# Forty early expert groups instead of forty-four, an earlier A load, and seam arithmetic on VectorE, in a two-block network with dense experts

## The chip, the cores and the metric

The kernel runs on one core of one Trainium2 chip. The metric is device microseconds of one execution. All matrix products are float32 work done as three products of rounded float32 parts (high and low halves), so that each weight tile costs a split into two tiles before it can be multiplied.

## What is computed

Two residual blocks over 512 tokens of width 1024. Each has a token mixer (gated linear attention in the first; retention and stick-breaking attention in the second) and then a PEER layer: eight heads pick 16 of 16,384 single-neuron experts by product keys. Cut to what matters here:

```python
def peer(h, w_query, sub_keys, expert_down, expert_up):          # second block; the first is alike
    qry = (ht @ w_query).reshape(T, 8, 2, 128)
    sub_scores = einsum('thpc,hpkc->thpk', qry, sub_keys)
    top_s, top_i = top_k(sub_scores, 16)                          # per half key
    best_s, best_c = top_k(all sums of two halves, 16)            # 16 experts per head
    gate = softmax(best_s)
    a = einsum('pd,ped->pe', x, expert_down[ids])                 # "U" products
    return einsum('pe,ped->pd', gelu(a) * gate, expert_up[ids])   # "V" products
```

Between the blocks stand two RMS norms with gains, and the second block's norms are modulated by scale, shift and gate rows that come from a small product of a condition vector.

## The kernel before

**The experts.** The first 128 tokens fetch their chosen rows: GpSimd issues 256 indirect DMAs of 128 rows (`Gathered.fetch`, L864), 128 of U and 128 of V, and VectorE consumes each with one 128x1024 operation (`Gathered.use`, L876 for U, L883 for V). The other 384 tokens are computed densely over all experts. The experts stand in 128 tiles of 128, taken in 64 pairs ("expert groups" of `GRP` = 2). For each tile, TensorE makes 24 matmuls of 128x384 into `pu` (`Inward.run`, L908), ScalarE takes the GELU of it into `A` (L915), and later A times the gate matrix `G`, which gives `W` (L1102 on VectorE), weighs the V rows: 36 matmuls of 128x512 for a pair into six accumulators `acc` (`mm3`, L119 to L121).

**Two stages.** In the early stage VectorE picks the experts and builds one-hot matrices, from which TensorE makes the gate matrix (`oh`, `og`, `pg`), in 32 steps for each of three token tiles. Between these steps TensorE runs U products: `PICK_MM`, `QUAD_MM` or `LAST_MM` matmuls at each step. `NEARLY` of the 64 pairs have their U products there, and their A tiles are written to DRAM (`ad`). In the dense stage, iteration p multiplies pair p. Pairs whose A came early are loaded back (`load_a(p + LA)`, L1071). The other pairs ("fresh" ones) get their U products in the dense stage, eight matmuls after each of the six parts of the iteration p for which p + 2 is fresh; since 144 of these matmuls (`OVER`, three pairs' worth) are done ahead, the last three fresh iterations find nothing left to multiply. The gathers left over are spread over the dense stage by weights: an iteration with p + 2 fresh counts `FW` = 4, another 1, up to pair 57.

**What sets the order.** Instructions are issued in the order of the code, one queue per engine. Weights and rows come by DMAs that SP issues in order, each behind the release of the buffer it fills; at most eight of SP's transfers are under way in the program's own semaphores, since each also waits for the eighth before it. `A` has 12 buffers (`GRP * AB`). ScalarE makes each high half, VectorE each low half (L264 for U, L1088 for V and W).

**The seams.** Between the dense stage of the first block and the second block's first products, `Between.rows` norms each token tile twice (L1731 to L1745); between the second mixer and its experts, `add` (L1796, L1797) and `rms_rows` (L197, L199) do the same; at the end `Last.rows` (L1829, L1833) adds the residual. GpSimd does some of the elementwise operations of these, chosen by `HGP`, `SHB`, `SHP` and the half; it also takes every power of -0.5. In iteration 33 of the first block the modulation table goes through DRAM (`modd`, L1708) and is read back as rows (L1565) on SP's queue.

Of the kernel before, what the change touches and what calls it, by code (L numbers as in the profile page):

```python
# [17 lines left out]
ALU = mybir.AluOpType  # L18
# [5 lines left out]
NT = 4  # L24
# [8 lines left out]
JUMPS = (16, 8, 5, 4, 3, 2, 2, 2)  # L33
SUBE = lambda nc: nc.vector
GRP = 2
NEARLY = 44
NHELD = 0
FRONT = 4
MLAG = 1
# [9 lines left out]
MT = 16  # L49
FW = 4  # L50
WB = (0, 2)
LA = 2
AB = FRONT + 2
HGP = (0, 1, 2)
ADA = (8, 7, 7)
ADA0 = 0
SHB = (0,)
HALVES = ((0, 512), (512, 1024))
S1 = 2
YR = 2  # L60
# [14 lines left out]
M2_LAG = 4  # L75
SB = 1
SPE = 0
SHP = 3
RP_ACT = (0, 1)
PICK_MM = 40  # L80
QUAD_MM = 20
LAST_MM = 16
PK = 2
LAG = 3
DOT = (2, 2, 1)
# [7 lines left out]
class K:  # L93
# [83 lines left out]
    def rms_rows(self, pool, t, row, gain, out=None, shift=None, known=None):  # L177

        nc = self.nc
        rs = pool.tile([128, 1], F32, name=f"rs{t}", tag="rrs", bufs=NT)
        j = pool.tile([128, D], F32, name="rsj", tag="rsj", bufs=1)
        o = 512 if known is not None else 0
        self.square_mean(rs, j[:, o:], row[:, o:])
        yield
        if known is None:
            nc.vector.tensor_scalar(rs, rs, EPS, None, op0=ALU.add)
        else:
            nc.vector.scalar_tensor_tensor(rs, rs, EPS, known, op0=ALU.add, op1=ALU.add)  # L190
        nc.gpsimd.tensor_tensor(rs, rs, self.mhalf, op=ALU.pow)
        if out is None:
            out = pool.tile([128, D], F32, name=f"xn{t}", tag="xn", bufs=NT)
        yield
        for c in HALVES:
            c = slice(*c)
            nc.vector.scalar_tensor_tensor(out[:, c], row[:, c], rs, gain[:, c], op0=ALU.mult, op1=ALU.mult)  # L197
            if shift is not None:
                (nc.gpsimd if t < SHP else nc.vector).tensor_tensor(out[:, c], out[:, c], shift[:, c], op=ALU.add)  # L199
        yield  # L200
        self.turn(out, t)

# [1338 lines left out]
def body(tc, a, out, stop=None):  # L1541
    nc = tc.nc
    with ExitStack() as ctx:
        k = K(ctx, tc, a)
        c = k.const
# [55 lines left out]
        with ExitStack() as c1:  # L1601
# [40 lines left out]
            gf = gain_row(ada, a["norm_f_g"], "gf")  # L1642
# [6 lines left out]
            h = [pool.tile([128, D], F32, name=f"h{t}") for t in range(NT)]  # L1649
# [24 lines left out]
        sh = []  # L1674
# [37 lines left out]
        class Between:  # L1712
# [14 lines left out]
            def rows(self, t, parts):  # L1727
                h, n = self.h[t], D // len(parts)
                for i, p in enumerate(parts):
                    s = h[:, i * n:(i + 1) * n]  # L1730
                    nc.vector.tensor_tensor(s, s, p, op=ALU.add)  # L1731
                yield
                v = ada.tile([128, 2], F32, name="v", tag="v", bufs=NT)
                k.square_mean(v[:, 0:1], self.junk, h)
                hg = self.tile("wide")
                (nc.gpsimd if t in HGP else nc.vector).tensor_tensor(hg, h, gf, op=ALU.mult)
                yield
                k.square_mean(v[:, 1:2], self.junk, hg)
                yield
                nc.vector.tensor_scalar(v[:, 0:1], v[:, 0:1], EPS, None, op0=ALU.add)  # L1740
                nc.vector.scalar_tensor_tensor(v[:, 1:2], v[:, 0:1], EPS, v[:, 1:2], op0=ALU.mult, op1=ALU.add)
                nc.gpsimd.tensor_tensor(v, v, k.mhalf.to_broadcast([128, 2]), op=ALU.pow)
                yield
                nc.vector.scalar_tensor_tensor(h, hg, v[:, 1:2], cs, op0=ALU.mult, op1=ALU.mult)
                (nc.gpsimd if t in SHB else nc.vector).tensor_tensor(h, h, sh[0], op=ALU.add)  # L1745
                yield
                if t == 0:
                    yield
                k.turn(h, t)
                self.out.append((t, hg, v))  # L1750
# [18 lines left out]
        with ExitStack() as c1:  # L1769
            mp = pool_of(c1, "mp2")  # L1770
            MH = mp.tile([128, NK, T], F32R, name="MH")
            ML = mp.tile([128, NK, T], F32R, name="ML")
            cos, sin = mp.tile([128, T], F32, name="cos"), mp.tile([128, T], F32, name="sin")
            rv = [mp.tile([128, 512], F32, name=f"rv{t}") for t in range(NT)]
            for t, p in end.first:
                by = lambda x: x.rearrange("p (h d) -> p h d", h=8)
                nc.vector.tensor_tensor(by(rv[t]), by(p), grow[:, t, :, None].to_broadcast([128, 8, 64]), op=ALU.mult)
            ms.close()
            with ExitStack() as c3:
                pool = pool_of(c3, "mx2")  # L1780
                prod = Product(k, ws, 28, MH, ML, OUT_ORDER)
                mixer2(k, c3, pool, rv, cos, sin, MH, ML, ws, prod)
            ms.enter_context(tc.manual_schedule())
            pool = pool_of(c1, "po2")
            h = [pool.tile([128, D], F32, name=f"h{t}") for t in range(NT)]
            hn = pool_of(c2, "gt2", side="right").tile([128, D], F32, name="ghn")
            for t in range(NT):
                nc.sync.dma_start(h[t], x2[t])
            g1, shift, scale = (row(pool.tile([128, D], F32, name=f"row{i}"), i) for i in (2, 3, 4))
            steps = Steps()  # L1790

            def add(half):
                def f(t, p):
                    c_ = slice(half * 512, (half + 1) * 512)
                    m = pool.tile([128, 512], F32, name="m", tag="m", bufs=2)
                    nc.vector.tensor_tensor(m, p, g1[:, c_], op=ALU.mult)  # L1796
                    (nc.vector if half else nc.gpsimd).tensor_tensor(h[t][:, c_], h[t][:, c_], m, op=ALU.add)  # L1797
                    if half:
                        steps.add(k.rms_rows(pool, t, h[t], scale, hn if t == 0 else None, shift, k.half_mean(pool, t, h[t][:, :512])))
                        steps.step()  # L1800
                return f

            for _ in prod.parts([3]):
                pass
            for t in range(NT):
                add(0)(t, prod.outs[t])
            ws.ready(33)
            ah = Ahead(k, a["peer_w_query_2"], a["peer_sub_keys_2"], a["peer_down_2"], 4)
            token_rows(k, ws, 32, MH, ML, ["acc", "acc", "mm", "mm"], add(1), tail=True, order=OUT_ORDER)
            first = by_halves(k, ah.ws, steps)  # L1810
            for t in range(NT):
                nc.sync.dma_start(x3[t], h[t])

        class Last:
# [10 lines left out]
            def rows(self, t, parts):  # L1825
                y, n = self.tile("wide"), D // len(parts)
# [3 lines left out]
                yield  # L1830
                for i in range(2):
                    s = slice(i * 512, (i + 1) * 512)
                    (nc.vector if t == NT - 1 or i else nc.gpsimd).tensor_tensor(y[:, s], y[:, s], self.h[t][:, s], op=ALU.add)  # L1833
                    nc.sync.dma_start(out[t * 128:(t + 1) * 128, s], y[:, s])

            def close(self, steps):
# [109 lines left out]
```

## Time and profile before

| | |
|---|---|
| median of 3 runs | 3200.78 us (3193.4 to 3206.52) |
| the profiled execution | 3198.14 us |
| its span, first to last instruction | 3196.4 us |
| TensorE (PE) busy | 3085.1 us, 97% |
| VectorE (DVE) busy | 2559.8 us, 80% |
| mean granted TensorE clock | 0.987 |

The times of single instructions below are of the profiled execution, so sums are made against 3198.14 us; the span leaves 1.7 us around it. Matmuls are pipelined: what one costs is the distance between two starts, not the length that a row gives. The granted clock is a share of full speed (2.4 GHz; the other level is 1.2 GHz).

### The profile page before, as it was taken

Reading aid. Unit: us, or ns where it says so; the run is one execution under the profiler, and the core shown is the slowest. Engines: PE = TensorE matmul, PEld = TensorE weight load, DVE = VectorE, ACT = ScalarE, POOL = GpSimd, SP = SyncE. Lnnn points to the kernel's source line nnn. Section 1 sums busy time; section 2 is a strip of 40 time slices with the busy share of each in tenths; the row PEclk is TensorE's granted clock in tenths of the full one; section 3 lists DMA queues with packets and bytes.
Section 4 is the critical chain, followed back from the end, with each engine's and each line's share of the span. In section 5 each row is a group of like instructions: output and inputs, shape, how many; then the busy total and the mean of one; then the engine's idle time right before and its main releaser. Section 6 shows DMA issues by size and latency. Waiting matters only on the chain.

```text
span 3196.4 us, 45048 instructions
## 1 busy us (share of the span) xinstructions
PE 3085.1 (97%) x16481; PEld 2681.8 (84%) x16481; DVE 2559.8 (80%) x4759; ACT 1350.6 (42%) x1913; POOL 990.7 (31%) x780
## 2 busy tenths in 40 slices
PE   7999999999999999999999999999999999999998
PEld 5777789999988777887777777899999888888876
DVE  6776788888968888888766858888889688888886
ACT  3543334655643333333344642246556433333322
POOL 0442221222414444444212321012224154444441
PEclk9999999999999999999999999999999999999999
DMA  7113346888999999989832132368889999999896
GB/s 277 66 60 126 132 147 210 275 284 287 370 326 356 358 363 345 343 330 342 300 104 86 50 119 88 109 210 274 286 284 369 320 357 357 352 344 352 334 339 224
DMA packets 340735, 819.23 MB, mean 256 GB/s; under 512 B 29920, under 2 KB 173728, under 8 KB 340256
## 3 DMA queue, kind: packets, MB, share of 16 engines
q1 hardware_dynamic: 264016, 544.84, 48.3%
q0 software_dynamic: 73728, 268.47, 22.7%
q10 hardware_dynamic: 2768, 3.04, 0.3%
q8 instruction: 129, 2.11, 0.3%
q14 instruction: 94, 0.77, 0.1%
HBM read 720.79 MB, written 93.35 MB: 255 GB/s over the span
## 4 chain that ended last, share of the span: by engine, by line
PE 54%; issue 17%; DVE 14%; POOL 9%; ACT 3%; DMA 3%; POOLq 0%; SPq 0%; ACTq 0%; DVEq 0%
PE pu L908 26%; POOL gr L864 8%; PE pc L328 5%; PE pg L1042 3%; DVE gacc L883 3%; DVE VL L1088 2%; PE qy L121 2%; PE tr L120 2%; PE tr L121 2%; PE qy L120 2%; PE tr L119 2%; PE acc L120 2%; PE acc L121 2%; PE acc L119 2%; DVE uL L264 2%
## 5 line engine op out<-in xcount | busy, mean ns | idle before, releaser
L908 PE MATMUL pu<-XH,uL 128*128 128x384 f32 x2048 | 697.1, 340 | 9.2 <-DVE uL L264 8.9
L908 PE MATMUL pu<-XH,uH 128*128 128x384 f32 x2048 | 696.7, 340 | 2.1 <-ACT uH L254 2.1
L908 PE MATMUL pu<-XL,uH 128*128 128x384 f32 x2048 | 696.1, 340 | 0.0
L119 PE MATMUL acc<-VH,WH 128*128 128x512 f32 x1536 | 608.7, 396 | 28.2 <-ACT WH L1082 18.8
L120 PE MATMUL acc<-VL,WH 128*128 128x512 f32 x1536 | 604.9, 394 | 12.0 <-DVE VL L1088 11.8
L121 PE MATMUL acc<-VH,WL 128*128 128x512 f32 x1536 | 607.2, 395 | 0.0
L264 DVE TENSOR_TENSOR uL<-sr,uH 128x1024 fp32r<-128x1024 f32 x360 | 449.8, 1253 | 162.7 <-ACT uH L254 159.3
L254 ACT ACTIVATE uH<-sr 128x1024 fp32r<-128x1024 f32 x360 | 378.9, 1054 | 135.8 <-PE tr L121 81.9
L1082 ACT ACTIVATE WH<-W 128x384 fp32r<-128x384 f32 x256 | 134.3, 524 | 706.2 <-DVE W L1102 706.1
L908 PEld LDWEIGHTS pu<-XH,uL 128*128 128x128 f32 x2048 | 386.0, 188 | 16.0 <-DVE uL L264 11.7
L908 PEld LDWEIGHTS pu<-XH,uH 128*128 128x128 f32 x2048 | 386.0, 188 | 6.5 <-ACT uH L254 2.8
L908 PEld LDWEIGHTS pu<-XL,uH 128*128 128x128 f32 x2048 | 386.2, 189 | 4.2
L119 PEld LDWEIGHTS acc<-VH,WH 128*128 128x128 f32 x1536 | 291.1, 189 | 101.2 <-ACT WH L1082 36.9
L864 POOL DMA_INDIRECT gr<-in_peer_down_rows_dram,gid x128 | 198.3, 1549 | 571.8 <-DVE gr L876 394.4
L1088 DVE TENSOR_TENSOR VL<-vr,VH 128x1024 fp32r<-128x1024 f32 x256 | 315.1, 1231 | 55.8 <-ACT VH L1082 55.0
L864 POOL DMA_INDIRECT gr<-in_peer_u_rows_dram,gid x128 | 198.0, 1547 | 502.0 <-DVE gr L876 408.3
L121 PEld LDWEIGHTS acc<-VH,WL 128*128 128x128 f32 x1536 | 291.1, 190 | 71.4 <-DVE WL L1088 11.7
L120 PEld LDWEIGHTS acc<-VL,WH 128*128 128x128 f32 x1536 | 291.3, 190 | 71.1 <-DVE VL L1088 18.1
L883 DVE SCALAR_TENSOR_TENSOR gacc<-gr,ga,gacc 128x1024 f32<-128x1024 f32 x254 | 325.9, 1283 | 1.8
L915 ACT ACTIVATE A<-pu 128x384 f32<-128x384 f32 x256 | 127.0, 496 | 470.8 <-PE pu L908 466.7
L876 DVE SCALAR_TENSOR_TENSOR gr<-gr,ghn 128x1024 f32<-128x1024 f32 x256 | 310.4, 1218 | 0.0
L1088 DVE TENSOR_TENSOR WL<-W,WH 128x384 fp32r<-128x384 f32 x256 | 143.0, 559 | 160.5 <-ACT WH L1082 159.9
(402 smaller groups left out, 4840.1 us busy)
## 6 DMA issues: line engine op xcount, KB each, us to landing
sr<-in_peer_u_dram SPq DMA_DIRECT2D x128, 512.0 KB
vr<-in_peer_v_dram SPq DMA_DIRECT2D x128, 512.0 KB
sr<-in_peer_down_dram SPq DMA_DIRECT2D x128, 512.0 KB
vr<-in_peer_up_dram SPq DMA_DIRECT2D x128, 512.0 KB
gd<-st SPq DMA_DIRECT2D x96, 512.0 KB
G<-gd SPq DMA_DIRECT2D x64, 768.0 KB
ad<-A SPq DMA_DIRECT2D x176, 192.0 KB
A<-ad SPq DMA_DIRECT2D x176, 192.0 KB
```

Of the source, the lines that this page charges most:

```text
L119: mm(out, lH, rH, start=start, stop=False)
L120: mm(out, lH, rL, start=False, stop=False)
L121: mm(out, lL, rH, start=False, stop=stop)
L254: nc.scalar.activation(H, raw, AF.Copy)
L264: self.K_.nc.vector.tensor_tensor(L, raw, H.bitcast(F32), op=ALU.subtract)
L328: K_.nc.tensor.matmul(p, w[:, s], x[:, k, :], start=k == 0 and i == 0, stop=k == NK - 1 and i == 2)
L864: self.K_.nc.gpsimd.indirect_dma_start(out=r, out_offset=None, in_=self.V if v else self.U, in_offset=bass.IndirectOffsetOnAxis(ap=self.id ...
L876: nc.vector.scalar_tensor_tensor(r, r, 1.0, self.hn, op0=ALU.mult, op1=ALU.mult, accum_out=w)
L883: nc.vector.scalar_tensor_tensor(self.acc, r, w, self.acc, op0=ALU.mult, op1=ALU.add)
L908: nc.tensor.matmul(self.p[:, :TD], w, x, start=i == 0, stop=i == 23)
L1082: nc.scalar.activation(part[0], src, AF.Copy)
L1088: nc.vector.tensor_tensor(L, src, H.bitcast(F32), op=ALU.subtract)
```

## The change

Forty pairs instead of 44 have their U products in the early stage, so 24 instead of 20 are fresh. Fresh pairs before are 0, 1, 2, 3, 5, 8, 12, 16, 20, 23, 27, 31, 35, 38, 42, 46, 50, 53, 57 and 61; now they are 0, 1, 2, 3, 5, 8, 11 and every third from there to 62. The early stage makes 36, 18 or 15 U matmuls in a step instead of 40, 20 or 16. Eight A tiles fewer go to DRAM and come back in each block. An A tile is loaded three iterations ahead of its pair instead of two, in the same 12 buffers. Seventeen elementwise operations of the seams that GpSimd did go to VectorE; the powers stay on GpSimd.

```diff
-NEARLY = 44
+NEARLY = 40
-LA = 2
+LA = 3
-PICK_MM = 40
-QUAD_MM = 20
-LAST_MM = 16
+PICK_MM = 36
+QUAD_MM = 18
+LAST_MM = 15
@@ rms_rows (SHP = 3 is gone)
-                (nc.gpsimd if t < SHP else nc.vector).tensor_tensor(out[:, c], out[:, c], shift[:, c], op=ALU.add)
+                nc.vector.tensor_tensor(out[:, c], out[:, c], shift[:, c], op=ALU.add)
@@ Between.rows (HGP = (0, 1, 2) and SHB = (0,) are gone)
-                (nc.gpsimd if t in HGP else nc.vector).tensor_tensor(hg, h, gf, op=ALU.mult)
+                nc.vector.tensor_tensor(hg, h, gf, op=ALU.mult)
-                (nc.gpsimd if t in SHB else nc.vector).tensor_tensor(h, h, sh[0], op=ALU.add)
+                nc.vector.tensor_tensor(h, h, sh[0], op=ALU.add)
@@ add, second block
-                    (nc.vector if half else nc.gpsimd).tensor_tensor(h[t][:, c_], h[t][:, c_], m, op=ALU.add)
+                    nc.vector.tensor_tensor(h[t][:, c_], h[t][:, c_], m, op=ALU.add)
@@ Last.rows
-                    (nc.vector if t == NT - 1 or i else nc.gpsimd).tensor_tensor(y[:, s], y[:, s], self.h[t][:, s], op=ALU.add)
+                    nc.vector.tensor_tensor(y[:, s], y[:, s], self.h[t][:, s], op=ALU.add)
```

SP's queue in the first block, iterations 32 and 33 and the start of 34, before. `vr` is a V load, `sr` a U load, `A<-ad` a pair's A tiles, and the three `modd` rows are the modulation table's write and its two reads.

```order
L1071 DMA A<-ad 128x384 x2
L1076 DMA vr<-in_peer_v_dram 128x1024 x2
L1065 DMA G<-gd 128x1536
L239 DMA sr<-in_peer_u_dram 128x1024
L1076 DMA vr<-in_peer_v_dram 128x1024
L239 DMA sr<-in_peer_u_dram 128x1024
L1076 DMA vr<-in_peer_v_dram 128x1024
L1708 DMA modd<-aw 48x128
L1565 DMA cs<-modd 128x1024
L1565 DMA aw<-modd 128x1024
L1071 DMA A<-ad 128x384 x2
L1076 DMA vr<-in_peer_v_dram 128x1024 x2
```

The same queue from the start of iteration 33 in the changed kernel:

```order
L1068 DMA A<-ad 128x384 x2
L1062 DMA G<-gd 128x1536
L1073 DMA vr<-in_peer_v_dram 128x1024
L236 DMA sr<-in_peer_u_dram 128x1024
L1073 DMA vr<-in_peer_v_dram 128x1024
L236 DMA sr<-in_peer_u_dram 128x1024
L1705 DMA modd<-aw 48x128
L1562 DMA cs<-modd 128x1024
L1562 DMA aw<-modd 128x1024
L1068 DMA A<-ad 128x384 x2
L1073 DMA vr<-in_peer_v_dram 128x1024 x2
```

What moved: the A tiles of pair 36 stood behind the three `modd` rows and now stand ahead of them, at the head of iteration 33; behind them now stand those of pair 37.

VectorE's queue at the seam between the blocks, before, from the first tile's residual sum (L1731) on. `vr<-gr,gf` (L1736) and `gr<-gr,aw` (L1745) of this tile are on GpSimd's queue.

```order
L1731 TENSOR_TENSOR gr<-gr,gacc 128x1024
L1088 TENSOR_TENSOR WL<-W,WH 128x384
L1088 TENSOR_TENSOR VL<-vr,VH 128x1024
L1102 TENSOR_TENSOR W<-A,G 128x384
L1088 TENSOR_TENSOR WL<-W,WH 128x384
L1740 TENSOR_SCALAR v<-v 128x1
L1741 SCALAR_TENSOR_TENSOR v<-v 128x1
L1744 SCALAR_TENSOR_TENSOR gr<-vr,v,cs 128x1024
L1088 TENSOR_TENSOR VL<-vr,VH 128x1024
L264 TENSOR_TENSOR uL<-sr,uH 128x1024 x2
```

The same place in the changed kernel:

```order
L1728 TENSOR_TENSOR gr<-gr,gacc 128x1024
L1085 TENSOR_TENSOR WL<-W,WH 128x384
L1733 TENSOR_TENSOR vr<-gr,gf 128x1024
L1085 TENSOR_TENSOR VL<-vr,VH 128x1024
L1099 TENSOR_TENSOR W<-A,G 128x384
L1085 TENSOR_TENSOR WL<-W,WH 128x384
L1737 TENSOR_SCALAR v<-v 128x1
L1738 SCALAR_TENSOR_TENSOR v<-v 128x1
L1741 SCALAR_TENSOR_TENSOR gr<-vr,v,cs 128x1024
L1742 TENSOR_TENSOR gr<-gr,aw 128x1024
L1085 TENSOR_TENSOR VL<-vr,VH 128x1024
L261 TENSOR_TENSOR uL<-sr,uH 128x1024 x2
```

What moved: the gain product stands ahead of the first VL, and the shift add ahead of the last VL, which TensorE's last pair needs.

## Rows read from the trace of the kernel before

**Rows 1.** Part 1 of the page: busy time of each engine, its share of the span and its instructions.

```profile
PE 3085.1 (97%) x16481; PEld 2681.8 (84%) x16481; DVE 2559.8 (80%) x4759; ACT 1350.6 (42%) x1913; POOL 990.7 (31%) x780
```

**Rows 2.** The view by windows, whole stages of the two blocks: each row is a stretch in us from the span's start, its length, then busy us (and instructions begun) of PE, PEld, DVE, ACT and POOL, then the granted clock, the DMA share and GB/s. 530 to 930 is the early stage of the first block from the second token tile on, 930 to 1590 its dense stage; 2530 to 3170 is the dense stage of the second block.

```profile
530.00:660.00 130.00, 130.00 (x911) 125.41 (x910) 113.32 (x225) 75.95 (x94) 25.38 (x16) 1.00 0.83 274
...
790.00:895.00 105.00, 105.00 (x764) 100.38 (x763) 97.30 (x140) 63.47 (x74) 48.08 (x31) 1.00 1.03 367
895.00:930.00 35.00, 33.18 (x186) 31.87 (x185) 15.16 (x16) 15.16 (x22) 0.00 (x0) 1.00 0.92 326
930.00:1250.00 320.00, 308.49 (x1406) 256.57 (x1405) 266.22 (x373) 108.11 (x148) 136.90 (x92) 1.00 0.93 349
1250.00:1480.00 230.00, 225.66 (x1033) 190.24 (x1032) 191.96 (x212) 76.67 (x107) 101.01 (x72) 0.99 0.91 338
1480.00:1590.00 110.00, 102.42 (x428) 81.10 (x427) 88.97 (x102) 35.40 (x49) 32.67 (x25) 0.97 0.87 317
...
2530.00:2850.00 320.00, 319.20 (x1488) 274.24 (x1487) 266.60 (x363) 113.40 (x155) 146.28 (x99) 1.00 0.92 346
...
3065.00:3170.00 105.00, 97.63 (x401) 76.92 (x400) 83.18 (x95) 33.60 (x46) 30.74 (x24) 0.95 0.85 309
```

**Rows 3.** The timeline of PE, two neighbouring instructions in the early stage and three in the dense stage: start, modelled length, line, result and operands. The distance of two starts is what one matmul costs.

```profile
470.11 0.34 PE L908 MATMUL pu<-XH,uL 128*128 128x384 f32 x1
470.28 0.34 PE L908 MATMUL pu<-XH,uH 128*128 128x384 f32 x1
...
2753.11 0.34 PE L908 MATMUL pu<-XL,uH 128*128 128x384 f32 x1
2753.29 0.39 PE L119 MATMUL acc<-VH,WH 128*128 128x512 f32 x1
2753.51 0.39 PE L120 MATMUL acc<-VL,WH 128*128 128x512 f32 x1
```

**Rows 4.** The view of who waited for whom on DVE, 920 to 1560 us (dense stage, first block): us in total, times, longest.

```profile
DVE WL L1088 <- ACT WH L1082: 74.9, 118, 3.3
...
DVE W L1102 <- DMA A<-ad: 8.8, 3, 4.2
```

**Rows 5.** The timeline of DVE in a stretch of the dense stage without U products: start, length, line, operation; in brackets the idle time before.

```profile
1482.35 0.55 DVE L1102 TENSOR_TENSOR W<-A,G 128x384 f32<-128x384 f32 x1
...
1483.97 1.28 DVE L883 SCALAR_TENSOR_TENSOR gacc<-gr,ga,gacc 128x1024 f32<-128x1024 f32 x1
1485.16 1.22 DVE L1088 TENSOR_TENSOR VL<-vr,VH 128x1024 fp32r<-128x1024 f32 x1
...
1486.30 1.28 DVE L883 SCALAR_TENSOR_TENSOR gacc<-gr,ga,gacc 128x1024 f32<-128x1024 f32 x1
```

**Rows 6.** The view by tile of the gathered rows `gr`, 920 to 1560 us: the gathers issued in the dense stage, with their number and ns (least, median, most).

```profile
L864 POOL DMA_INDIRECT gr<-in_peer_v_rows_dram,gid x128: 934/1317/2147, 1138.5 to 1550.6; - x128
...
L864 POOL DMA_INDIRECT gr<-in_peer_u_rows_dram,gid x60: 933/1678/1987, 934.4 to 1136.2; - x60
```

**Rows 7.** The timeline after the modulation table's round trip through DRAM (first block): the A loads as SP issues them, then the DVE product that waits for them and the matmul that waits behind.

```profile
1312.87 1.28 SPq L1071 DMA_DIRECT2D A<-ad  x2
...
1320.09 0.56 DVE L1102 TENSOR_TENSOR W<-A,G 128x384 f32<-128x384 f32 x1 [4.20 <-DMA A<-ad]
...
1322.20 0.50 PE L119 MATMUL acc<-VH,WH 128*128 128x512 f32 x1 [1.75 <-ACT VH L1082]
```

**Rows 8.** The view by windows, the ten microseconds of that wait (columns as in rows 2).

```profile
1320.00:1330.00 10.00, 7.20 (x24) 5.32 (x24) 8.35 (x10) 3.89 (x5) 2.85 (x2) 0.83 0.89 339
```

**Rows 9.** The timeline near the end of the dense stage, first block: gathered rows on DVE, the product behind them, and the matmul that waits.

```profile
1499.26 2.60 DVE L883 SCALAR_TENSOR_TENSOR gacc<-gr,ga,gacc 128x1024 f32<-128x1024 f32 x2
...
1501.78 0.55 DVE L1102 TENSOR_TENSOR W<-A,G 128x384 f32<-128x384 f32 x1
...
1503.89 0.51 PE L119 MATMUL acc<-VH,WH 128*128 128x512 f32 x1 [1.70 <-ACT VH L1082]
```

**Rows 10.** The view of who waited for whom on DVE, 530 to 660 us (early stage, second token tile).

```profile
DVE oh L1022 <- PE pg L1042: 11.8, 16, 2.6
```

**Rows 11.** The timeline of DVE in the early stage, fourth token tile: the starts of one step with a U split (840.95 to 844.57) and of one without (844.57 to 847.20).

```profile
840.95 0.69 DVE L1022 TENSOR_TENSOR oh<-iota,idx 128x1024 f16<-128x1024 f16 x1 [0.78 <-PE pu L908]
...
844.57 0.68 DVE L1022 TENSOR_TENSOR oh<-iota,idx 128x1024 f16<-128x1024 f16 x1
...
847.20 1.23 DVE L264 TENSOR_TENSOR uL<-sr,uH 128x1024 fp32r<-128x1024 f32 x1
```

**Rows 12.** The timeline of the seam between the blocks: GpSimd's two pieces of arithmetic and what stood on DVE and PE beside and behind them.

```profile
1591.15 2.60 POOL L1736 TENSOR_TENSOR vr<-gr,gf 128x1024 f32<-128x1024 f32 x1 [39.57 <-DVE gr L1731]
...
1591.42 3.41 DVE L1088 TENSOR_TENSOR VL<-vr,VH 128x1024 fp32r<-128x1024 f32 x1
...
1599.30 3.30 POOL L1745 TENSOR_TENSOR gr<-gr,aw 128x1024 f32<-128x1024 f32 x1 [1.40 <-DVE gr L1744]
...
1600.41 0.50 PE L120 MATMUL acc<-VL,WH 128*128 128x512 f32 x1 [2.01 <-DVE VL L1088]
```

**Rows 13.** The timeline of the seam ahead of the second block's early stage: the low halves of the second token tile, and the query product that waits for them.

```profile
1932.10 1.27 DVE L168 TENSOR_TENSOR XL<-xt,XH 128x512 fp32r<-128x512 f32 x2
...
1932.83 0.58 PE L120 MATMUL qy<-XL,uH 128*128 128x256 f32 x1 [0.61 <-DVE XL L168]
```

**Rows 14.** The view by line, DVE's own adds of 128x512 in that seam: ns least, median, most.

```profile
L1797 DVE TENSOR_TENSOR h<-h,m x4: 691/692/1041, 1916.9 to 1925.0; 128x512 f32<-128x512 f32 x4
```

More of the change, by code (lines that the diff above doesn't have):

```diff
@@ L51 @@
 WB = (0, 2)
-LA = 2
+LA = 3
 AB = FRONT + 2
-HGP = (0, 1, 2)
 ADA = (8, 7, 7)
 ADA0 = 0
-SHB = (0,)
 HALVES = ((0, 512), (512, 1024))
@@ L77 @@
 SPE = 0
-SHP = 3
 RP_ACT = (0, 1)
-PICK_MM = 40
-QUAD_MM = 20
-LAST_MM = 16
+PICK_MM = 36
+QUAD_MM = 18
+LAST_MM = 15
 PK = 2
```

## The prediction

> **What bounds the kernel now.** I read the page's busy times first: TensorE is busy for 97% of the span and VectorE for 80% [rows 1]. No change of order removes TensorE's work, so I looked, stage by stage, for the microseconds in which it stands still or runs at a lower clock [rows 2]. In the early stage it is busy for every microsecond from 530 to 895, while VectorE has 13% to spare at first and 7% in the fourth token tile. In the first block's dense stage it loses 11.5 us of 320, then 4.3 of 230, then 7.6 of 110. The second block's dense stage loses 0.8 of its first 320 us, and 7.4 of 105 in its end. The seams lose the rest.
>
> Next I asked who makes it wait there. VectorE never rests for want of work in the dense stage: its idle time is nearly all a wait of 0.63 us (74.9 us in 118 times) for ScalarE's high half, which follows each product W, and 8.8 us for A tiles that land late [rows 4]. So the dense stage is a race of two engines. One iteration costs TensorE 36 matmuls of 128x512 at 0.22 to 0.23 us, 8.1 us; a fresh one has 48 U matmuls of 0.177 more, 16.6 us [rows 3]. On VectorE a W with its low half takes 1.62 us, a gather's use 1.19, a V split 1.14 [rows 5]. Two of the first and last are 5.5 us; the gathers come on top.
>
> The code has 190 gathers left for the dense stage, and the rows show 188 of them after 920 us [rows 6]. Up to pair 57 there are 43 plain iterations that count 1 and 15 fresh ones that count 4, so 103 shares: 1.84 gathers in a plain iteration and 7.4 in a fresh one. VectorE then needs 5.5 + 2.2 = 7.7 us against 8.1 in a plain one, and 5.5 + 8.8 + 2.3 for two U splits = 16.6 against 16.6 in a fresh one. That is a tie. Where the first block adds a modulation product (one 128x1024 operation, about the 1.2 us of a V split, in every other iteration up to 25) VectorE loses the race; the second block has none and hardly stalls.
>
> **The change part by part.** *Moving four pairs* takes 8 x 24 matmuls, at 0.177 us 34 us, out of each early stage and puts them into the dense stage, where they cost the same [rows 3]: nothing by itself. What counts is what either stage makes of it.
>
> *Early stage.* The cover is VectorE's lead. In the second tile a step loses two U matmuls, 11.3 us over 32 steps, and VectorE loses 2.7 U splits, about 2.6 us. VectorE waited there 11.8 us for TensorE [rows 10], so it still has about 3 us left. In the fourth tile VectorE's step takes 3.62 us with a U split and 2.63 without [rows 11]; 16 of 24 steps have one, which makes 3.29, about TensorE's own 105/32 = 3.28 [rows 2]. Now it is 3.25 against 3.10: VectorE falls behind by 0.15 x 32 = 5 us over the tile. It enters the tile up to three steps (`LAG`), some 10 us, ahead, and TensorE then has 35 us in which VectorE is busy only 15 [rows 2], so most of that is hidden. With no lead, each block would pay 5 us here and about 4 in the first tile's picking (11 steps that shrink by 0.7 us for TensorE and by 0.2 for VectorE), 9 in all. The bounds are 0 and 9; I take 1.2 for each block, near the rows with a wait for TensorE: **+2.4**.
>
> *Dense stage, VectorE's load.* There are now 39 plain and 19 fresh iterations, 115 shares: 1.65 and 6.6 gathers. VectorE needs 7.5 us against 8.1, and 15.7 against 16.6. With modulation products at 0.6 us an iteration it was 8.3 and 17.2, behind in both; it becomes 8.1 and 16.3, level or ahead. Of the 11.5 us from 930 to 1250 [rows 2] I expect 2 to stay: **-9.5** (bounds -3 and -11.5). In the second block little was lost: **-1**.
>
> *A three iterations ahead.* After the modulation table's round trip, SP issues pair 36's A tiles at 1312.87, and W waits 4.20 us for them at 1320.09, TensorE 1.75 at the first matmul after and more behind it [rows 7]. Those ten microseconds are 2.8 short and at a clock of 0.83, another 1.7 of work [rows 8]. In the new queue these loads stand ahead of the table, in iteration 33. With the 0.6 us ahead of it that is **-5** (bounds -1 and -6); other A waits [rows 4] lie in the -9.5. The 12 buffers suffice: at most three pairs loaded and four computed ahead, of which one is always both. V loads queued behind are no later than now. The rest of that stretch gives **-0.5**.
>
> *The end of the dense stage.* Iterations 51 and 55 fetch at weight 4 with no U products left. VectorE needs 5.5 + 7.4 x 1.19 = 14.3 us there against TensorE's 8.1; two gathers in a row stand ahead of the product W, and TensorE waits [rows 9]. Now it is iterations 54 and 57, with 6.6 gathers each: 0.9 us shorter, four times, **-3**. The stalls stay otherwise, and so does their clock (0.97 and 0.95 [rows 2]). Bounds: nothing, and -14 if the slack gained before gives VectorE a lead.
>
> *Seams.* At the seam between blocks the gain product on GpSimd (2.60 us) stretches VectorE's V split beside it to 3.41 us [rows 12], against 1.22 elsewhere [rows 5]. On VectorE the product costs 1.14, so the next W comes 1.05 us earlier. But the shift add, which GpSimd ran after VectorE had gone on, now stands ahead of the last V split, on which TensorE waits at 1600.41 [rows 12]: that gives the 1.05 and 0.1 more back. Two more gain products for the later tiles stand in VectorE's queue: +0.5. In the other seam six adds of about 0.62 us (0.69 long [rows 14]) come into VectorE's queue ahead of the second tile's low halves, on which the first query product waits [rows 13]: +3.7 at most, less what GpSimd no longer stretches (an add took 1.04 once [rows 14]); I take +1.5. At the very end VectorE has four adds after the last product instead of three: +0.6, less a little gained before. Together **+2.5**, bounds -5 and +6.
>
> The Trainium skill (SBUF — State Buffer, Who interferes with whom) says that a VectorE instruction with two inputs in SBUF and a GpSimd instruction that reads SBUF lock each other out for a whole instruction. The stretched split agrees: 2.2 us for a neighbour of 2.60. It speaks for a larger gain than mine, the second rival's.
>
> The sum against the profiled execution: 3198.1 + 2.4 - 9.5 - 1 - 5 - 0.5 - 3 + 2.5 = **3184 us**. The median of the runs is 2.6 us above that execution, so this is 0.5% below the median.
>
> **The rivals.**
>
> *No change.* The early stage's end pays about what the dense stage gains: VectorE's lag costs 4 us a block, modulation stalls fall by 4 only since transfers keep their rate (349 GB/s [rows 2]), and A gives 3: 3198.1 + 8 - 4 - 3 - 1 + 2.5 = 3200; with a little more gain 3190. For it: VectorE is as short in the fourth tile as in the dense stage [rows 2, 11]. Against it: the 35 us of cover.
>
> *GpSimd's lock.* If every piece of GpSimd arithmetic held VectorE as the first did [rows 12], 17 pieces (an estimate from rows 12: four at 2.6 to 3.3 and thirteen at half of that, 28 us) would be bought for 14 us on VectorE, and perhaps half of the difference lies on the path: 3184 - 2.5 - 7 = 3174. Against it: the piece of 3.30 us ends beside VectorE's work at no visible wait of TensorE but the one that stays.
>
> *The end's stalls go too.* With VectorE ahead, all 17.5 us of the first block's earlier losses and two thirds of the 23 us in the two ends (7.6 + 7.4 idle, 8 by the clock [rows 2]) vanish: 3198.1 - 17.5 - 1 - 15 + 4.9 = 3170. Against it: the buffers let VectorE lead by no more than about half an iteration, and 5 us are missing at once.
>
> *Slower.* VectorE becomes the bound of the early stage: it enters the fourth tile without a lead, and TensorE waits at each `pg` and each U split. This decides once VectorE's lag there passes its 10 us lead. It costs 9 us in each block; with seams at +6 and half the gains (-9.5), 3198.1 + 18 + 6 - 9.5 = 3213. The gathers' transfers, at a DMA share of 1.03 in that tile [rows 2], would be the reason for the missing lead.
>
> **How the numbers follow.** The forecast (3175 to 3194) has 0.45, no change 0.25, the end's stalls 0.15, the lock 0.05, slower 0.10. A measurement of this kernel can tell about 0.5% from no change, 16 us: below 3184.8 lie half of the forecast's case, the third rival and the lock, 0.44; above 3216.8 next to nothing but part of the slower case, to which I add what I have not seen, 0.08; 0.48 is between. The range from 3164 to 3204 leaves out the slower case and the far ends.
>
> **What would show it.** Right: in the first block's dense stage, waits of W for A gone, TensorE's loss ahead of the stage's end down from 16 us to under 5 over a stage 34 us longer, no clock of 0.83 behind the modulation table, and early windows with TensorE still full. The two stalls near the end stay, three iterations apart. The qy product at the second seam starts a microsecond later relative to the sums. Wrong: idle TensorE in the fourth tile with waits for `og` or U splits; late V loads behind A loads; or the dense stage's waits for W unchanged although fewer gathers stand in each iteration.

## The result, and the profile after

| | before | after |
|---|---|---|
| median of 4 runs in one set | 3198.64 us (3193.4 to 3206.52) | 3148.11 us (3144.83 to 3154.27) |
| ratio, 95% interval | | 0.9842 [0.9816, 0.9868] |
| the profiled execution / its span | 3198.14 / 3196.4 us | 3154.27 / 3152.6 us |

The change gives 50 us, more than three times the forecast, and the time lies below the range. The profiled execution after is the longest of its four runs, so the two profiles differ by 43.8 us of span; the steps below are summed to that.

Part 1 of the page after, to be held against [rows 1]: the work is the same 16481 matmuls, but TensorE's busy time itself is 21.4 us shorter. That is the first hint at what the prediction misread.

```profile
PE 3063.7 (97%) x16481; PEld 2684.1 (85%) x16481; DVE 2558.1 (81%) x4776; ACT 1353.9 (43%) x1913; POOL 935.8 (30%) x763
```

The view by windows after, stages as in [rows 2] and the ten microseconds of [rows 8], columns as there. 500 to 860 is the first block's early stage, 900 to 1560 its dense stage, 2470 to 3130 the second block's.

```profile
500.00:630.00 130.00, 130.00 (x877) 126.04 (x876) 120.08 (x229) 74.95 (x95) 24.03 (x18) 1.00 0.81 263
760.00:860.00 100.00, 99.43 (x716) 93.88 (x714) 98.57 (x147) 60.88 (x70) 44.97 (x31) 1.00 1.02 363
900.00:1220.00 320.00, 319.92 (x1503) 276.32 (x1502) 271.57 (x378) 113.93 (x155) 140.19 (x93) 1.00 0.96 359
1220.00:1440.00 220.00, 220.00 (x1044) 191.59 (x1043) 186.62 (x207) 79.37 (x109) 92.90 (x67) 1.00 0.93 344
1440.00:1560.00 120.00, 116.71 (x515) 96.30 (x514) 96.30 (x109) 38.78 (x53) 40.55 (x28) 0.99 0.85 305
1283.00:1293.00 10.00, 10.00 (x51) 8.98 (x50) 9.27 (x10) 4.09 (x6) 4.72 (x4) 1.00 1.02 409
2470.00:2790.00 320.00, 320.00 (x1510) 278.36 (x1509) 260.06 (x355) 115.18 (x158) 135.16 (x94) 1.00 0.93 340
3010.00:3130.00 120.00, 117.08 (x518) 96.83 (x517) 94.17 (x107) 39.82 (x54) 39.69 (x28) 0.99 0.84 308
```

In the dense stage TensorE now hardly stands still before the end, and the stretch behind the modulation table is full, at a clock of 1.00 (before 7.20 of 10 us at 0.83). The early stage is still full (99.43 of 100 us) although VectorE is busy for 98.6 of 100 us in the fourth tile.

The view of who waited for whom on DVE, 890 to 1530 us after, the two longest rows: the waits for ScalarE have no 3.3 us among them any more, and W's wait for A [rows 4] has no row at all.

```profile
DVE WL L1085 <- ACT WH L1079: 69.9, 118, 0.7
DVE VL L1085 <- ACT VH L1079: 18.6, 45, 1.2
```

**How much TensorE loses, by starts.** The view by tile gives the first and the last start of `acc`, first block, before and then after:

```profile
L119 PE MATMUL acc<-VH,WH x768: 387/389/793, 928.0 to 1609.0; 128*128 128x512 f32 x192
L121 PE MATMUL acc<-VH,WL x768: 387/389/632, 928.5 to 1609.4; 128*128 128x512 f32 x192
```

```profile
L116 PE MATMUL acc<-VH,WH x768: 388/389/628, 895.8 to 1579.9; 128*128 128x512 f32 x192
L118 PE MATMUL acc<-VH,WL x768: 388/389/747, 896.3 to 1580.4; 128*128 128x512 f32 x192
```

Between them stand 2304 `acc` at 0.227 us and, before, 624 `pu` at 0.176 (the distances of full stretches, [rows 3]): 632.8 of 681.4 us, so **48.6 us are lost**. After, 828 `pu`: 668.7 of 684.5, so **15.8**. For the second block the same view gives 661.5 and 679.5 us, so 28.7 and 10.8. These figures hold waits and stretches at the lower clock together. Taken iteration by iteration from the starts in the timeline of PE (us lost, before → after; by its way of counting, the totals differ from those above by up to 0.2):

| iterations | first block | second block |
|---|---|---|
| 0 to 34 | 20.9 → 1.6 | 3.3 → 0 |
| 35, 36 (behind the modulation table) | 6.5 → 0.1 | 0.7 → 0 |
| 37 to 50 | 2.0 → 0.3 | 3.0 → 0 |
| 51 to 57 (bursts) | 12.8 → 0.1 | 14.5 → 0 |
| 58 to 62 (the burst of 57) | 0.4 → 6.5 | 0 → 5.9 |
| 63 (the last pair) | 6.0 → 7.2 | 7.5 → 5.1 |

Against this, the prediction read 11.5, 4.3 and 7.6 us of idle time in the first block and 0.8 and 7.4 in the second; the 215 us between these last two it did not read (2.0 idle, 4.9 lost by starts). The timelines of PE and of its weight loads (PEld) before show where the rest hid, at one of the small stalls of the second block:

```profile
2783.55 0.19 PEld L121 LDWEIGHTS acc<-VH,WL 128*128 128x128 f32 x1
2783.77 0.39 PE L121 MATMUL acc<-VH,WL 128*128 128x512 f32 x1
2784.43 0.19 PEld L119 LDWEIGHTS acc<-VH,WH 128*128 128x128 f32 x1 [0.69 <-ACT WH L1082]
2784.43 0.50 PE L119 MATMUL acc<-VH,WH 128*128 128x512 f32 x1 [0.27 <-ACT WH L1082]
2784.53 0.19 PEld L120 LDWEIGHTS acc<-VL,WH 128*128 128x128 f32 x1
2784.76 0.40 PE L120 MATMUL acc<-VL,WH 128*128 128x512 f32 x1
2785.02 0.19 PEld L121 LDWEIGHTS acc<-VH,WL 128*128 128x128 f32 x1 [0.29 <-DVE WL L1088]
2785.02 0.50 PE L121 MATMUL acc<-VH,WL 128*128 128x512 f32 x1
2785.36 0.34 PE L908 MATMUL pu<-XH,uH 128*128 128x384 f32 x1
```

From 2783.77 to 2785.36 stand four `acc` matmuls, worth 0.91 us, in 1.59: 0.68 lost. The view shows 0.27 idle. The wait for WH in fact costs 0.43: the modelled end of a matmul lies 0.39 us after its start, the next full-pace start only 0.227. The rest stands in the three distances behind it, 0.33, 0.26 and 0.34. The weight loads tell them apart: there are two waits, the second (0.26) for VectorE's WL, which PE's own rows don't show, and behind each the next start comes 0.1 us late.

The Trainium skill (Perfetto Trace Analysis, Identifying the Most-Contended Engine) calls matmul busy time a bad measure, since matmuls are pipelined, and asks for the busy share of the weight loads. Here that share shows the loss: before, it is 256.57 of 320 us in the first block's dense stage against 274.24 in the second's, whose iterations have the same matmuls [rows 2]. That is 17.7 us less, where the starts say 17.2 and the idle time 10.7. The page has pipelined matmuls look smaller in a trace than they are; here the modelled length is larger than the cost (0.39 us for 0.227), and the measurement decides.

### The profile page after: what moved, and what is told of

The parts are those of the page before. It is cut to its first block, busy times and chain, and to the rows that moved or that the text cites. A ratio compares the mean times of both kernels' runs of the same rounds, so it can differ in the third digit from the quotient of the medians.

```text
span 3152.6 us, 44942 instructions
## 1 busy us (share of the span) xinstructions
PE 3063.7 (97%) x16481; PEld 2684.1 (85%) x16481; DVE 2558.1 (81%) x4776; ACT 1353.9 (43%) x1913; POOL 935.8 (30%) x763
## 4 chain that ended last, share of the span: by engine, by line
PE 57%; issue 17%; DVE 13%; POOL 9%; DMA 2%; ACT 1%; SPq 0%; POOLq 0%; ACTq 0%; DVEq 0%
PE pu L905 22%; POOL gr L861 8%; PE pc L325 5%; PE acc L117 4%; PE acc L118 4%; PE acc L116 4%; DVE uL L261 3%; DVE gr L873 2%; PE pg L1039 2%; PE tr L117 2%; PE tr L118 2%; PE tr L116 2%; PE qy L118 2%; PE qy L117 2%; PE qy L116 2%
## 5 line engine op out<-in xcount | busy, mean ns | idle before, releaser
L905 PE MATMUL pu<-XH,uH 128*128 128x384 f32 x2048 | 706.4, 345 | 0.0
L116 PE MATMUL acc<-VH,WH 128*128 128x512 f32 x1536 | 601.7, 392 | 4.5 <-ACT VH L1079 3.5
L1085 DVE TENSOR_TENSOR VL<-vr,VH 128x1024 fp32r<-128x1024 f32 x256 | 312.7, 1221 | 48.2 <-ACT VH L1079 47.1
L861 POOL DMA_INDIRECT gr<-in_peer_down_rows_dram,gid x128 | 185.6, 1450 | 558.3 <-DVE gr L873 383.5
L861 POOL DMA_INDIRECT gr<-in_peer_u_rows_dram,gid x128 | 188.8, 1475 | 472.9 <-DVE gr L873 383.4
L1079 ACT ACTIVATE VH<-vr 128x1024 fp32r<-128x1024 f32 x256 | 268.0, 1047 | 13.4 <-PE acc L118 6.3
```

The costliest lines, as they stand in the source:

```text
L116: mm(out, lH, rH, start=start, stop=False)
L861: self.K_.nc.gpsimd.indirect_dma_start(out=r, out_offset=None, in_=self.V if v else self.U, in_offset=bass.IndirectOffsetOnAxis(ap=self.id ...
L905: nc.tensor.matmul(self.p[:, :TD], w, x, start=i == 0, stop=i == 23)
L1079: nc.scalar.activation(part[0], src, AF.Copy)
L1085: nc.vector.tensor_tensor(L, src, H.bitcast(F32), op=ALU.subtract)
```

## The experiments

Loss is TensorE's loss in the two dense stages by starts, as above. "Before" ran again in each of the three sets: 3199.45, 3201.27 and 3199.09 us.

| run | median us | ratio to before, 95% | loss, first block | second |
|---|---|---|---|---|
| before | 3199 | | 48.5 | 28.9 |
| after | 3148.11 | 0.9842 [0.9816, 0.9868] | 15.7 | 11.0 |
| e1, forty pairs alone | 3157.73 | 0.9864 [0.9848, 0.9880] | 23.9 | 11.5 |
| e2, A three ahead alone | 3192.56 | 0.9976 [0.9966, 0.9986] | 42.0 | 27.7 |
| e3, seams alone | 3203.98 | 1.0018 [1.0007, 1.0028] | 48.2 | 28.9 |
| e4, after with A two ahead | 3158.71 | 0.9868 [0.9851, 0.9884] | 22.2 | 12.1 |
| e5, after without the last burst | 3138.44 | 0.9802 [0.9786, 0.9819] | 9.1 | 4.8 |
| e6, after with 143 ahead | 3163.81 | 0.9881 [0.9865, 0.9898] | 19.6 | 17.2 |
| e7, before without bursts | 3184.24 | 0.9946 [0.9931, 0.9961] | 39.6 | 23.6 |
| e8, before, short modulation | 3186.07 | 0.9958 [0.9941, 0.9975] | 36.7 | 27.4 |
| e9, before, short gather use | 3142.79 | 0.9810 [0.9794, 0.9826] | 8.9 | 7.5 |
| e10, e5 with GpSimd's seams | 3136.47 | 0.9807 [0.9794, 0.9821] | 7.3 | 6.5 |
| e11, e5 again | 3138.32 | 0.9809 [0.9795, 0.9822] | 9.2 | 5.0 |
| e12, e5 with 36 pairs | 3166.59 | 0.9894 [0.9879, 0.9910] | 8.2 | 8.2 |

**The three parts of the change, each alone.**

```diff
 e1, before with
-NEARLY, PICK_MM, QUAD_MM, LAST_MM = 44, 40, 20, 16
+NEARLY, PICK_MM, QUAD_MM, LAST_MM = 40, 36, 18, 15
 e2, before with
-LA = 2
+LA = 3
 e3, before with the five lines of the seams as in the change
 e4, after with
-LA = 3
+LA = 2
```

> The kernel before with the forty early pairs alone (step counts 36, 18, 15); A still loaded two iterations ahead, GpSimd keeps its arithmetic at the seams. I count TensorE's loss in a dense stage as the distances between starts of neighbouring matmuls above 0.227 us (acc) and 0.176 us (pu): 48.5 and 28.9 us before, 15.7 and 11.0 after. Theory V (fewer gathers in each iteration free VectorE): nearly all of it comes from the pairs, the loss in the first block is about 22 with one wait of 6 us for A after the modulation table, in the second about 11, the time 3152 to 3160. Rival L (A tiles that land late held the stage, so loading them earlier is what counts): this kernel keeps most of the loss, 35 or more in the first block, 3175 to 3190.

> The kernel before with A loaded three iterations ahead and nothing else changed. Theory V: only the 6.5 us that stand in iterations 35 and 36, behind the modulation table, go; 3190 to 3195, the second block's loss stays 28 to 29. Rival L: the small losses of iterations 10 to 33 go as well, loss in the first block under 30, 3175 or less.

> The kernel before with the seventeen operations on VectorE and nothing else changed. By my sum of the prediction: 2.5 us longer, 3199 to 3203, the loss of the last pair (iteration 63) in the first block grows by about 1 us from 6.0 and the seam between the second mixer and its experts by about 2. Rival (GpSimd's arithmetic held VectorE): 5 to 12 us shorter, 3187 to 3194.

> The changed kernel with A loaded two iterations ahead again. Theory V: the wait behind the modulation table returns and costs 3 to 7 us, 3151 to 3155; nothing in the second block changes. Rival L: 10 us or more, spread over both dense stages. Third possibility: VectorE's lead now hides the late A tiles, within 1 us of the changed kernel.

The pairs alone give 42 us, nearly the whole (theory V). Of e1's loss, 6.8 us stand in iterations 0 to 34 and 2.8 behind the table, where I had expected about 6. A three ahead alone gives 7: the loss in iterations 35 and 36 falls from 6.5 to 1.2, and iterations 0 to 34 give 4.3, more than theory V allowed. Undone in the changed kernel it costs 7.6 us by starts, of which 5.4 stand in iterations 0 to 34 and 3.8 in 35 and 36 (the end gives some back); the whole time differs by 10.6, from two sets of runs. That is more than the 3 to 7 that theory V allowed, and by the time alone rival L's case; but the second block loses only 1.1 more, so the loss is not spread over both stages as that rival had it. The wait of W for A in the dense stage of the first block, view of who waited for whom, e1 and e4:

```profile
DVE W L1102 <- DMA A<-ad: 11.6, 9, 4.5
```

```profile
DVE W L1099 <- DMA A<-ad: 11.4, 7, 4.6
```

With fewer gathers and A two ahead, W waits longer for A than before (8.8, [rows 4]), most likely since VectorE comes earlier and finds A not there; that was not taken apart. So late A tiles are a second limit behind VectorE's load, in the first block only (e1's second block loses 11.5, as after). The seams alone cost 4.5 us (2 to 9 by the interval): the forecast of +2.5 is within it, the rival that GpSimd's arithmetic held VectorE has the wrong sign.

**Is it VectorE's time, or the gathers' transfers?** Fewer gathers in an iteration mean both. e9 leaves the transfers and shortens VectorE's part; e8 does so for the modulation products, which only the first block has.

```diff
 e8, ada_block (in the dense stage, and 22 products ahead of the first mixer)
-scalar_tensor_tensor(raw, raw, 1.0, cs, ...)
+scalar_tensor_tensor(raw[:, :128], raw[:, :128], 1.0, cs[:, :128], ...)
 e9, Gathered.use in the dense stage
-scalar_tensor_tensor(r, r, 1.0, self.hn, ...)
+scalar_tensor_tensor(r[:, :128], r[:, :128], 1.0, self.hn[:, :128], ...)
-scalar_tensor_tensor(self.acc, r, w, self.acc, ...)
+scalar_tensor_tensor(self.acc[:, :128], r[:, :128], w, self.acc[:, :128], ...)
```

> The kernel before; VectorE's modulation products in the dense stage of the first block take 128 of 1024 columns, so seven eighths of each sum are left out; their transfers stay. Theory (these products cost VectorE the race in the first block): the loss of iterations 0 to 34, 20.9 us before, falls to that of the second block, 3.3, and the whole first block's from 48.5 to about 31; 3178 to 3186. Rival (the transfers or the U rows' consumption make the difference between the blocks): first block's loss stays over 42, 3193 or more.

> The kernel before; in the dense stage each gathered row's use on VectorE takes 128 of 1024 columns, so seven eighths of the first token tile's sums from there on are left out; all gathers and transfers stay. Theory V (VectorE's time for the gathers sets the stalls): the loss in iterations 0 to 62 falls from 42 to under 10 (the wait for A behind the table stays) in the first block and from 21 to under 2 in the second, the bursts near the end included; 3140 to 3152. Rival D (the gathers' transfers, or their landing, set the stalls): less than 15 us are gained.

In e9 the loss before the last pair falls from 42.5 to 7.3 us and from 21.4 to 1.2, with no gather fewer. The windows of e9, the stretches of the first block's dense stage that answer to [rows 2]:

```profile
935.00:1255.00 320.00, 320.00 (x1496) 275.84 (x1495) 197.06 (x395) 115.51 (x158) 129.62 (x101) 1.00 0.98 375
1255.00:1485.00 230.00, 228.95 (x1060) 195.52 (x1059) 133.25 (x223) 79.78 (x110) 84.85 (x74) 1.00 0.94 354
```

DMA moves more than before (375 against 349 GB/s) and TensorE is full: rival D falls, VectorE's time for the gathers is the cause. Only behind the last burst something stays (4.7 of the 7.3 us in iterations 51 to 57), where transfers that come in a row may count too; that was not taken apart. In e8 iterations 0 to 34 of the first block lose 11.6 us instead of 20.9; I had expected 3.3. (The edit also shortens 22 such products ahead of the first mixer, so e8 is read by this loss and not by its whole time.) The modulation products are half of what sets the blocks apart. What stays stands beside waits of W for A of 10.8 us in that stage, the limit that e1 and e4 show too.

**The bursts at the end.**

```diff
 e5, after with
-weights = [FW if p + 2 >= FRONT and fresh(p + 2) else 1 ...]
+weights = [FW if p + 2 >= FRONT and fresh(p + 2) and p < 55 else 1 ...]
 e7, before with the same line, p < 50
 e6, after with
-PICK_MM = 36
+PICK_MM = 37
```

> The changed kernel, in which iterations 57 and 60 (fresh by their number, but with no U products left) count 1 and not 4 in the spreading of the gathers, so 112 shares and 1.70 or 6.8 gathers. Theory (the one stall left is the burst of 6.6 gathers in iteration 57): the loss in iterations 58 and 59, 6.5 us in the first block and 5.9 in the second, goes and nothing else moves, 3133 to 3139. Rival (VectorE has no slack for the 0.05 and 0.2 gathers more in every other iteration): small losses come back through the stage, or the last pair's loss grows, and the time stays within 4 us of the changed kernel.

> The changed kernel with 37 instead of 36 U matmuls in a picking step, so that 11 more are done ahead and iteration 54 has one U matmul left instead of twelve (2.1 us of cover less at its burst of gathers). Theory (VectorE's lead hides that burst): the loss in iterations 54 to 56 stays under 1 us, time within 3 us of the changed kernel's 3148. Rival (the twelve U matmuls hid it): 2 to 9 us are lost in iterations 55 and 56 of each block, 3152 to 3166.

> The kernel before, in which iterations 51 and 55 (fresh without U products) count 1 and not 4: 97 shares, 1.96 and 7.8 gathers instead of 1.84 and 7.4. Theory V: the 12.8 and 14.5 us lost in iterations 52 to 57 go, but each plain iteration has 0.12 and each fresh one 0.4 gathers more, so the other losses (29.7 and 6.9 us without the last pair) grow by 5 to 15 us together; 3180 to 3190. Rival (the bursts are all there is): 3170 to 3175. Second rival (VectorE is short everywhere, and what is taken from the bursts is lost elsewhere): 3194 or more.

The timeline of DVE after, iteration 57: five gathered rows used around one V split ahead of the product W; and of PE, the matmul that waits behind.

```profile
1519.12 2.60 DVE L880 SCALAR_TENSOR_TENSOR gacc<-gr,ga,gacc 128x1024 f32<-128x1024 f32 x2
1521.64 1.22 DVE L1085 TENSOR_TENSOR VL<-vr,VH 128x1024 fp32r<-128x1024 f32 x1
1522.78 1.32 DVE L880 SCALAR_TENSOR_TENSOR gacc<-gr,ga,gacc 128x1024 f32<-128x1024 f32 x1
1524.26 2.61 DVE L880 SCALAR_TENSOR_TENSOR gacc<-gr,ga,gacc 128x1024 f32<-128x1024 f32 x2 [0.17 <-DMA gr<-in_peer_v_rows_dram,gid]
1526.79 0.55 DVE L1099 TENSOR_TENSOR W<-A,G 128x384 f32<-128x384 f32 x1
```

```profile
1526.67 0.39 PE L118 MATMUL acc<-VH,WL 128*128 128x512 f32 x1
1528.89 0.50 PE L116 MATMUL acc<-VH,WH 128*128 128x512 f32 x1 [1.83 <-ACT VH L1079]
```

Iteration 54 has the same burst and TensorE waits nowhere behind it. e6 says why: with one U matmul left there instead of twelve, 4.8 and 4.5 us are lost in iterations 55 and 56. The timeline of PE in e6:

```profile
1498.82 0.50 PE L116 MATMUL acc<-VH,WH 128*128 128x512 f32 x1 [1.21 <-ACT VH L1079]
1500.08 0.50 PE L117 MATMUL acc<-VL,WH 128*128 128x512 f32 x1 [0.76 <-DVE VL L1085]
1501.10 0.76 PE L116 MATMUL acc<-VH,WH 128*128 128x512 f32 x1 [0.30 <-ACT WH L1079]
```

My theory of a lead that hides the burst by itself fell; eleven U products, 1.9 us at 0.176, made the difference. e6 is 15.7 us longer than after, of which the starts explain 10.1; the sets differ. e5 takes the burst of iteration 57 away and loses nothing elsewhere but 1 us: 3138.44 us, as forecast, and below both kernels. e7 shows the same edit where VectorE has no slack: 25.7 of the bursts' 27.3 us go, and 12 come back as losses elsewhere (29.7 to 32.9 in the first block outside the bursts and the last pair, 6.9 to 15.8 in the second).

**How far the early stage can go, and the seams once more.**

```diff
 e10, e5 with the five lines of the seams as before the change
 e11, e5 unchanged
 e12, e5 with
-NEARLY, PICK_MM, QUAD_MM, LAST_MM = 40, 36, 18, 15;  p < 55
+NEARLY, PICK_MM, QUAD_MM, LAST_MM = 36, 32, 16, 14;  p < 57
```

> The kernel of e5 with GpSimd's arithmetic at the seams as before the change; compared with e5 again in the same set of runs. Theory (by the sum of the prediction, +2.5, and by e3, 4.5 longer): 2 to 5 us shorter than e5 again, 3133 to 3137, from the seam between the second mixer and its experts and from the last pair of the first block. Rival (once the stage's stalls are gone, VectorE at the seams is free): within 1.5 us of e5 again.

> The kernel of e5 unchanged, as the reference for the other runs of this set: 3135 to 3141.

> The kernel of e5 with 36 early pairs (step counts 32, 16, 14; iterations 58 and 60, fresh without U products, count 1). TensorE's work is the same. Theory of the early stage's lead: VectorE now lags by up to 9 us in the fourth tile against a lead of about 10, so each early stage costs 0 to 4 us, and the dense stage has nothing left to give but the last pair: 3137 to 3147. Rival (VectorE's lag is already at the limit and the early stage turns into VectorE's): 9 us or more for each block, 3155 to 3170. Second rival: the stage still gains, under 3135.

e10 and e11 can't be told apart (3132.8 to 3142.87 and 3133.14 to 3141.63), so the sign of the seams in this kernel stays open; they are worth at most a few us. e12 is 28 us slower than e5. From the first `pu` to the first `acc` its early stages take 426.7 and 427.9 us, 23 less than after, where 204 matmuls fewer at 0.176 are worth 35.9: they pay 12.7 and 12.4 us. The windows of e12 in the second, third and fourth token tile, and PE's longest wait from 446 to 740 us:

```profile
500.00:620.00 120.00, 117.78 (x813) 112.82 (x812) 116.86 (x229) 68.87 (x86) 27.32 (x19) 1.00 0.81 268
620.00:740.00 120.00, 117.06 (x858) 111.09 (x857) 112.69 (x225) 77.47 (x90) 27.27 (x19) 1.00 0.91 297
740.00:838.00 98.00, 95.27 (x697) 89.55 (x696) 94.78 (x141) 58.41 (x68) 44.78 (x32) 0.98 1.04 373
```

```profile
PE pu L905 <- DVE uL L261: 8.9, 7, 3.2
```

VectorE is now busy for 116.86 of 120 us in the second tile (after: 120.08 of 130), and TensorE waits for U splits (after, from 446 to 760 us: 3.8, 2 times): the slower case of the prediction, but four pairs later, and already in the second tile, where I had looked at the fourth.

## Why the prediction was wrong, point by point

The mechanism was right, the size was not. By starts, for the profiled execution (the early stage from the first `pu` to the first `acc`):

| term | forecast | measured |
|---|---|---|
| early stages | +2.4 | -0.5 (486.4 to 449.9, 487.2 to 451.4, against 35.9 of moved matmuls each) |
| VectorE's load, first block (0 to 34) | -9.5 | -19.3 |
| VectorE's load, second block (0 to 50) | -1 | -7.0 |
| A after the modulation table | -5 | -6.4 |
| the rest of that stretch | -0.5 | -1.7 |
| bursts at the end | -3 | -15.1 (-6.6 and -8.5) |
| seams, last pairs among them | +2.5 | +2.0 |
| sum | -14 | -48.0 |

The time up to the first `pu`, which the change doesn't touch, was 4.3 us longer in this execution, which makes -43.7 against 43.8 of span.

*The step that failed* is the first reading: the dense stage's loss was taken from idle time and clock. By starts, [rows 2]'s 11.5 us from 930 to 1250 are 19.0, the 4.3 to 1480 are 9.9, the 7.6 to 1590 are 12.9, and in the second block "0.8 of its first 320 us" are 1.8 and the end's 7.4 are 14.2. My bound of -11.5 was therefore no bound: 19.3 us went from iterations 0 to 34. The rows at 2784.43 show how: that small stall costs 2.5 times its idle time, the stretch from 930 to 1250, all at a clock of 1.00, 1.7 times. In the ends the lower clock, which the prediction did count, is part of the difference. In the second block the 215 us left unread hold 4.9 of the 7.0 us of the term.

*The second failure* is the term for the bursts. I took over the three fresh iterations without U products from before and forecast -3, where -15.1 was measured. The step counts 36, 18 and 15 make 2052 matmuls, 132 beyond forty pairs and not 144 (and 204 moved, not 192), so iteration 54 keeps twelve and the two stalls three iterations apart became one; e6, where one of the twelve is left, loses 4.8 and 4.5 us there again, so these products, on top of VectorE's slack, removed one burst's stall of each block. The prediction had not seen them: that part of the gain was luck. The third rival, that the end's stalls go too, was the nearest; of its reason against, that the buffers let VectorE lead too little, e6 shows that it held once the twelve were gone.

*VectorE's race* stands as told: e9 leaves its time as the cause, e7 shows that the losses move with its load, e1 that the pairs bring most. The modulation products explain only half of what sets the blocks apart (e8); late A tiles add to it. These other A waits did not lie in the load's term, as I had it: e1 and e4 keep them although the load is gone.

*A three iterations ahead* came about as forecast behind the table (-6.4 for -5, just past its bound of -6), and gave 4 to 5 us more in iterations 0 to 34 (e2, e4).

*The early stage* had cover, as argued, and cost nothing; e12 shows that its reserve ends within the next four pairs.

*Seams.* The timeline of DVE and PE after, where [rows 12] and [rows 13] stood:

```profile
1561.09 1.22 DVE L1733 TENSOR_TENSOR vr<-gr,gf 128x1024 f32<-128x1024 f32 x1
1562.22 1.22 DVE L1085 TENSOR_TENSOR VL<-vr,VH 128x1024 fp32r<-128x1024 f32 x1
...
1566.55 1.28 DVE L1741 SCALAR_TENSOR_TENSOR gr<-vr,v,cs 128x1024 f32<-128x1024 f32 x1 [0.85 <-POOL v L1739]
1567.87 1.23 DVE L1742 TENSOR_TENSOR gr<-gr,aw 128x1024 f32<-128x1024 f32 x1
1569.01 1.22 DVE L1085 TENSOR_TENSOR VL<-vr,VH 128x1024 fp32r<-128x1024 f32 x1
```

```profile
1570.28 0.80 PE L117 MATMUL acc<-VL,WH 128*128 128x512 f32 x1 [3.28 <-DVE VL L1085]
...
1906.01 0.58 PE L117 MATMUL qy<-XL,uH 128*128 128x256 f32 x1 [1.66 <-DVE XL L165]
```

The V split is 1.22 us again and not 3.41, but the gain product and the shift add stand ahead of the last one, and TensorE waits 3.28 instead of 2.01; the query product waits 1.66 instead of 0.61. Both as forecast. The rule of the Trainium skill (SBUF — State Buffer, Who interferes with whom) on VectorE and GpSimd is borne out by the one split, and not as a gain: taking GpSimd's arithmetic away cost 4.5 us alone (e3) and made no difference in e10 and e11.

## What to carry to other kernels

Where one engine is 97% busy, count what it loses by the distance of starts: the stage's length less so many instructions at their full-pace distance. Idle time understates short stalls of a pipelined engine: in the five stretches of [rows 2] that lie in dense stages it shows 31.6 us, and 57.8 were lost, of which at most 10 by the lower clock (by the granted clock of these rows). Before an edit that moves work between stages, recount what each iteration has left under every burst; eleven matmuls decided over 9 us of two blocks. And follow the gain until the giving stage runs out: forty pairs cost the early stage nothing, 36 cost it about 12.5 us a block.

## What the runs showed of the hardware that was not expected

A stall costs TensorE more than the wait, since the weight load of the waiting matmul stands still with it. At full pace a load begins one matmul ahead (2783.55 for the matmul at 2783.77). At 2784.43 and 2785.02 load and matmul begin together, and the next start comes 0.33 and 0.34 us later, not 0.227, at a granted clock of 1.00. That holds for the dense stages before as a whole: of the 90 `acc` matmuls at that clock, followed by another, that begin with their load, 79 are followed by the next start after 0.325 to 0.345 us; of the 4297 whose load began ahead, 4245 after 0.215 to 0.265. Pace is back after that one start (behind the wait at 1522.91 of the changed kernel the distances are 0.34, 0.24 and 0.23), unless a second wait follows, as that for WL does at 2785.02. That the load itself takes the 0.11 us was not tried apart.
